# The factors of the second and the final RMSNorm as rows through DRAM, in place of diagonals and products with ones

## The chip, the cores and the metric

The kernel runs on one core of a Trainium2 chip. The metric is the device time of one execution in microseconds (us), of which a median over several executions is given. The engines are named as in the profile: PE is TensorE (PEld its weight loads), DVE is VectorE, ACT is ScalarE, POOL is GpSimd, and SP is SyncE, which issues most of the DMA transfers.

## The reference

One layer for 2048 prompt tokens and 64 sample tokens of width 1024, all in float32. What matters here are the second and the final norm; the first half of the layer is cut to a line.

```python
def rmsnorm(x, g):
    xf = x.astype(jnp.float32)
    y = xf * lax.rsqrt(jnp.mean(xf * xf, -1, keepdims=True) + EPS)
    return y * g.astype(jnp.float32)

def layer(...):
    ...                       # norm 1, projection, pooling mixer and mLSTM, output projection
    x = x + gt1 * mix
    h2 = rmsnorm(x, g2) * (1 + sc2) + sh2
    up = h2 @ w_up
    ...                       # causal depthwise convolution of width 3, then
    x = x + gt2 * ((jax.nn.silu(g) * a) @ w_down)

y = rmsnorm(x, g_final)
```

Each norm has one factor for each token, the reciprocal root of a mean over the 1024 features.

## The kernel before

Activations lie with features on the 128 partitions and tokens along the free axis, so a norm's factor must be multiplied along the free axis, the same row on every partition. Products are made from float32 values split into a high and a low part, which is why a matmul often comes three times.

The first half of the layer goes over four token groups of 512 (the last has 576, with the sample tokens). In it a scheduler sets the order of each engine's instructions from the order in which they are written and their dependencies. The second half, the FFN, goes over three groups of 704 tokens, each seen as two halves of 352 (FH). There the order of PE, ACT, DVE and POOL is the order in which the instructions are written, and SP's is the scheduler's.

Side work is written as Python generators in lists (bg[0] to bg[4], and side). Each `yield` is a place to stop, and a product calls tick(0) twice, each call advancing the first generator by one step. A product of the FFN is twelve matmuls of 352 columns. So the number of yields sets where in the row of products a step of side work stands.

Every engine works its own row in order. A tile that two operations share makes the later one wait for the earlier.

The steps that the change and the prediction name:

- `rstd_rows` (the sum of squares turned into factors for token groups 0 to 2) and `stat2` with `rstd_cols` (for group 3) leave the second norm's factors as columns in RS2: 128 tokens on the partitions, one column for each tile of 128 tokens. `final` does the same for the final norm in RF, by `stat_cols`.
- `bcast_cols` turns columns into a row that stands on all partitions: DVE multiplies the identity by the factors (L687, L692), ACT and DVE split the result into a high and a low part (L696, L697), PE multiplies both by a matrix of ones, two matmuls for each 352 tokens (L702, L703), and ACT copies the result out of PSUM into rb (L704).
- `normed` multiplies by rb and the gain on DVE (L714) and adds the shift on ACT (L717).
- `norm_h` makes the normed input of FFN group 0 during the last token group: it loads x from DRAM (x2d, L727), in 16 pieces of 352 tokens, and stores the result (h2d). `prepare` does so for FFN groups 1 and 2, inside the FFN of the group before.
- `final` multiplies the eight tiles of a group's result by rb (L1911) and stores them to yT (L1915). `load_x2` (L1883) then refills these tiles from x2d for the next group, and the down-projection adds into them (L2010). The last group has its own ending, which the change leaves alone.
- Around norm_h, the last token group has `proj_v` (weights w_v, products L1129, evictions gt on DVE and va on ACT, both by a helper at L233), the work on w_ada (L210, on DVE) and the splitting of weights into high and low parts (L394 on ACT, L397 on DVE).
- In the FFN, L1595 is the up-projection, L1604 and L1608 take its results from PSUM, L1568 and L1573 are the convolution, L1642 and L1725 are other evictions on ACT, L2038 and L2161 are down-projections.

Of the kernel before, what the change touches and what calls it, by code (L numbers as in the profile page):

```python
# [9 lines left out]
F32 = mybir.dt.float32  # L10
# [55 lines left out]
def tile_layer(ctx: ExitStack, tc: tile.TileContext, xT, vecs, cst, rst, w_mod, w_ada, c_rows, w_qkou, w_v, w_pool,  # L66
# [443 lines left out]
    def rstd_rows(ssum, o, out, done):  # L510
# [18 lines left out]
        done.append(1)  # L529

# [26 lines left out]

    def modulate(dst, x, k, rb, G, sh, o):
# [12 lines left out]
    pool.memset(RS2, 0.0)  # L571
    RF = cp.tile([P, 6], F32, tag="RF", name="RF")
    pool.memset(RF, 0.0)
# [19 lines left out]
    def stat2(o, ssum):  # L593
        out = RS2[:, 4 * o.g:4 * o.g + len(o.chunks)]
        for _ in range(12):
            yield
        rstd_cols([ssum], o, out)
        yield

    def outproj(o, mix, between):  # L600
# [75 lines left out]
    def bcast_cols(rs, t0, w, box, scr, r0=0):  # L676

        rb = scr("rb")
        dg, dh, dl = scr(), scr(F32R), scr(F32R)
        t = t0  # L680
        while t < t0 + w:
            c, a = divmod(t, P)
            n = 1
            if a == 0 and t + P <= t0 + w:
                n = (t0 + w - t) // P
                v = dg[:, t - t0:t - t0 + n * P].rearrange("p (t c) -> p t c", c=P)
                dve.tensor_tensor(out=v, in0=ident.unsqueeze(1).broadcast_to([P, n, P]),  # L687
                                  in1=rs[:, c:c + n].unsqueeze(2).broadcast_to([P, n, P]), op=ALU.mult)
                t += n * P
            else:  # L690
                e = min(P, a + t0 + w - t)
                dve.tensor_scalar(out=dg[:, t - t0:t - t0 + e - a], in0=ident[:, a:e], scalar1=rs[:, c:c + 1],  # L692
                                  scalar2=None, op0=ALU.mult)
                t += e - a
        yield
        act.activation(dh[:, :w], dg[:, :w], AF.Copy)  # L696
        dve.tensor_tensor(out=dl[:, :w], in0=dg[:, :w], in1=dh[:, :w].bitcast(F32), op=ALU.subtract)  # L697
        yield
        yield
        for lo in range(0, w, FH):  # L700
            ps = m2_ps()
            pe.matmul(ps[:, :FH], ones_r, dh[:, lo:lo + FH], start=True, stop=False)  # L702
            pe.matmul(ps[:, :FH], ones_r, dl[:, lo:lo + FH], start=False, stop=True)  # L703
# [1612 lines left out]
```

## Time and profile before

| | |
|---|---|
| runs | 2162.03, 2164.13, 2164.81 us; median 2164.13 |
| the profiled execution's own time | 2170.81 us |
| its span | 2169.0 us |
| granted TensorE clock, mean | 0.998 |
| busy: PE, PEld | 2143.5, 2042.9 us |
| busy: DVE, ACT, POOL | 1629.1, 1096.2, 250.5 us |
| DMA | 543.63 MB, mean 251 GB/s |

Durations come from the profiled execution. A timeline's row has the start, the length, the engine, the line, what is written and read, a count, and in brackets the idle time before it with what ended it. A matmul's own duration is its latency; how much of PE's row it takes is read from the starts of its neighbours. DMA rows have the size of one transfer and the median time from issue to landing.

### The profile page before, as it was taken

How to read it: one execution, taken by the hardware profiler on the slowest of the kernel's cores; microseconds unless marked ns; L12 is line 12 of the kernel's file. 1: busy time of each engine (PE TensorE's matmuls, PEld its weight loads, DVE VectorE, ACT ScalarE, POOL GpSimd, SP SyncE). 2: the span in 40 equal slices, each digit the busy share in tenths (PEclk: the TensorE clock that was granted, in tenths of full speed). 3: DMA queues.
4: the chain of work that ended last, by engine and by line, in shares of the span. 5: the costliest groups of instructions: out<-in, count | busy, mean ns of one | idle time of the engine just before them, and what ended most of it. 6: DMA issues, size and time to landing. Idle time of an engine off the chain costs nothing.

```text
span 2169.0 us, 37946 instructions
## 1 busy us (share of the span) xinstructions
PE 2143.5 (99%) x13488; PEld 2042.9 (94%) x13488; DVE 1629.1 (75%) x3068; ACT 1096.2 (51%) x2182; POOL 250.5 (12%) x499
## 2 busy tenths in 40 slices
PE   8999999999999999999999999999999999999998
PEld 7788988888899999999999999999999999999998
DVE  5678768767964868797957668988876597887874
ACT  4555235334333546464736455655655365565554
POOL 0000000002000101010101120100100331111112
PEclk9999999999999999999999999999999999999999
DMA  8897998988886576889977976666678675555542
GB/s 306 305 327 256 336 338 279 354 319 292 279 306 221 168 261 219 303 279 313 331 225 244 322 265 196 229 224 199 221 232 264 217 260 183 174 174 189 174 160 79
DMA packets 245862, 543.63 MB, mean 251 GB/s; under 512 B 25252, under 2 KB 68772, under 8 KB 242856
## 3 DMA queue, kind: packets, MB, share of 16 engines
q1 hardware_dynamic: 236232, 518.89, 70.6%
q10 hardware_dynamic: 9440, 22.32, 2.6%
q8 instruction: 106, 1.74, 0.3%
q14 instruction: 84, 0.69, 0.1%
HBM read 415.12 MB, written 125.99 MB: 249 GB/s over the span
## 4 chain that ended last, share of the span: by engine, by line
PE 71%; DVE 8%; DMA 4%; issue 2%; ACT 2%; SPq 0%; POOL 0%; DVEq 0%; POOLq 0%; ACTq 0%
PE mm L1595 33%; PE mm L460 14%; PE mm L2161 12%; PE mm L2038 8%; DVE wt L397 2%; DMA wt<-wsum 1%; PE mm L1129 1%; DMA raw<-w_ada 1%; DVE tg L1573 1%; ACT tg L1568 0%; PE m L1350 0%; PE m L1330 0%; PE m L1352 0%; DVE scr L233 0%; DMA wsum<-w 0%
## 5 line engine op out<-in xcount | busy, mean ns | idle before, releaser
L1595 PE MATMUL mm<-hx,wt 128*128 128x352 f32 x5544 | 888.6, 321 | 1.6 <-DVE eg L1604 1.6
L1595 PEld LDWEIGHTS mm<-hx,wt 128*128 128x128 f32 x5544 | 881.9, 188 | 2.9 <-ACT wt L394 1.3
L460 PE MATMUL mm<-hl,wt 128*128 128x512 f32 (+2 forms) x1920 | 388.4, 357 | 0.8 <-ACT va L233 0.8
L394 ACT ACTIVATE wt<-raw 128x512 fp32r<-128x512 f32 (+3 forms) x470 | 276.8, 597 | 169.6 <-PE mm L2161 47.7
L460 PEld LDWEIGHTS mm<-hl,wt 128*128 128x128 f32 x1920 | 315.7, 189 | 43.9 <-ACT va L233 1.0
L397 DVE TENSOR_TENSOR wt<-raw,wt 128x512 fp32r<-128x512 f32 (+3 forms) x470 | 312.7, 671 | 47.8 <-ACT wt L394 47.0
L2161 PE MATMUL mm<-av,wt 128*128 128x448 f32 (+1 forms) x1632 | 262.7, 322 | 0.0
L2161 PEld LDWEIGHTS mm<-av,wt 128*128 128x128 f32 x1632 | 250.4, 188 | 11.1
L2010 DVE SCALAR_TENSOR_TENSOR x<-mm,MOD,x 128x352 f32<-128x352 f32 (+3 forms) x360 | 167.4, 504 | 78.6 <-PE mm L2161 65.1
L2038 PE MATMUL mm<-av,wt 128*128 128x352 f32 x1344 | 220.8, 323 | 2.5 <-DVE ea L1604 0.9
L2038 PEld LDWEIGHTS mm<-av,wt 128*128 128x128 f32 x1344 | 215.4, 188 | 5.6 <-DVE ea L1604 3.6
L1642 ACT ACTIVATE mm<-mm 128x352 f32<-128x352 f32 x196 | 87.8, 448 | 250.3 <-PE mm L1595 194.0
L460 PE MATMUL mm<-mx,wt 128*128 128x512 f32 (+1 forms) x960 | 183.1, 352 | 0.4 <-DVE scr L233 0.3
L460 PEld LDWEIGHTS mm<-mx,wt 128*128 128x128 f32 x960 | 159.4, 189 | 23.3 <-issue 0.5
L1573 DVE SCALAR_TENSOR_TENSOR ta<-ea,V,ta 128x704 f32<-128x704 f32 (+1 forms) x132 | 125.7, 952 | 64.4 <-ACT ta L1568 51.6
L1573 DVE SCALAR_TENSOR_TENSOR tg<-eg,V,tg 128x704 f32<-128x704 f32 (+1 forms) x132 | 125.7, 952 | 62.0 <-ACT tg L1568 59.7
L397 DVE TENSOR_TENSOR wt<-wt 128x512 fp32r<-128x512 f32 x196 | 132.8, 684 | 12.9 <-ACT wt L394 12.9
L394 ACT ACTIVATE wt<-wt 128x512 fp32r<-128x512 f32 x196 | 119.8, 623 | 36.2 <-DMA wt<-wsum 32.0
L1551 POOL COPY ea<-UC 128x2 f32<-128x2 f32 x66 | 32.9, 499 | 484.8 <-DVE ta L1573 397.0
L1782 ACT ACTIVATE tg<-tg 128x704 f32<-128x704 f32 (+1 forms) x66 | 52.5, 795 | 71.2 <-DVE tg L1573 71.2
L1129 PE MATMUL mm<-wt,hl 128*128 128x256 f32 (+1 forms) x576 | 71.1, 284 | 0.0
L1129 PEld LDWEIGHTS mm<-wt,hl 128*128 128x128 f32 x576 | 70.3, 190 | 0.6 <-issue 0.4
(298 smaller groups left out, 2173.5 us busy)
## 6 DMA issues: line engine op xcount, KB each, us to landing
wt<-wsplit SPq DMA_DIRECT2D x132, 512.0 KB, 4.5
raw<-w_up SPq DMA_DIRECT2D x198, 256.0 KB, 4.0
wt<-hl_kept SPq DMA_DIRECT2D x96, 512.0 KB, 5.9
wt<-wsum SPq DMA_DIRECT2D x132, 256.0 KB, 4.9
wsplit<-wt SPq DMA_DIRECT2D x66, 512.0 KB, 5.5
w<-w_up SPq DMA_DIRECT2D x44, 512.0 KB, 5.1
wsum<-w SPq DMA_DIRECT2D x22, 1024.0 KB, 4.8
Bd<-fscr ACTq DMA_DIRECT2D x56, 352.0 KB, 4.3
```

Of the source, the lines that this page charges most:

```text
L394: act.activation(u.w[:, 0, :u.n], u.raw[:, :u.n], AF.Copy)
L397: dve.tensor_tensor(out=u.w[:, 1, :u.n], in0=u.raw[:, :u.n], in1=u.w[:, 0, :u.n].bitcast(F32), op=ALU.subtract)
L460: pe.matmul(ps[bi][:, :hi - lo], U[:, a, k % 4 * P:(k % 4 + 1) * P], mv[k][:, b, lo:hi], start=(at == 0 and pi == 0), stop=(k == order[-1] ...
L1129: pe.matmul(ps[ti][:n, :cols], h[4 * kh + k4][:, b, lo:lo + n], U[:, a, k4 % 2 * cols:(k4 % 2 + 1) * cols], start=(kh == 0 and k4 == 0 and ...
L1551: pool.tensor_copy(ext[:, 0:2], UC[:, f, :])
L1573: dve.scalar_tensor_tensor(out=t[:, :E], in0=ext[:, j:j + E], scalar=wc(j, f), in1=t[:, :E], op0=ALU.mult, op1=ALU.add)
L1595: pe.matmul(bk.t[:, :FH], U[:, a, kc * P:(kc + 1) * P], Bo.at(nm, kc, b), start=(first and kc == 0 and pi == 0), stop=(kc == 3 and pi == 2 ...
L1642: act.activation(to.t[:, :FH], bk.t[:, :FH], AF.Copy)
L1782: act.activation(self.tg[:, :E], self.tg[:, :E], AF.Silu)
L2010: dve.scalar_tensor_tensor(out=x3[n][:, a:b], in0=bk.t[:, a - lo:b - lo], scalar=gt2(n, s), in1=x3[n][:, a:b], op0=ALU.mult, op1=ALU.add)
L2038: pe.matmul(bk.t[:, :FH], U[:, a, c:c + P], quad.put(op, m, b), start=(first and m == 0 and pi == 0), stop=(m == 1 and pi == 2), skip_grou ...
L2161: pe.matmul(bks[i].t[:, :hi - lo], U[:, a, k % 4 * P:(k % 4 + 1) * P], av[k][:, b, lo:hi], start=(k == 0 and (a, b) == PASSES[0]), stop=(k ...
```

## The change

The factors, as columns, are transposed by PE into a small tile with tokens along the free axis, copied out of PSUM by DVE and stored to DRAM by ACT's DMA queue (`row_out`). Where they are wanted, one DMA, issued by ACT, reads that row with stride zero into all 128 partitions (`spread_row`). Diagonals, splits, products with ones and the copies of their results go, and with them the two clears of RS2 and RF. `norm_h` is now advanced to its first yield before `proj_v` of the last token group; it waits three yields after its rows, as does `prepare`. `final` waits five yields between the store and the load, and five between the load and the first use.

```diff
...
                               op0=ALU.mult, op1=ALU.add)
             pool.tensor_tensor(out=out[:n, a:b], in0=out[:n, a:b], in1=half[:n, :b - a], op=ALU.pow)
         done.append(1)
+        if to is not None:
+            yield
+            yield
+            row_out(to, out, token_tiles(o), scr)
 
     def bcast(rs, o, box):
 
...
         box.append(rb)
         yield
 
+    def row_out(to, cols, tiles, new):
+
+        pt, R, t = m2_ps(), new(), 0
+        for i, (c, n, w) in enumerate(tiles):
+            pe.transpose(pt[:c, i * P:i * P + n], cols[:n, t:t + c], ident[:n, :n])
+            dve.tensor_copy(R[:c, i * P:i * P + n], pt[:c, i * P:i * P + n])
+            act.dma_start(out=to[w:w + c * n].rearrange("(c p) -> c p", p=n), in_=R[:c, i * P:i * P + n])
+            t += c
+
+    def token_tiles(o):
+        return [(b - a, n, a * P) for (a, b, n, s) in o.tsegs]
+
+    def spread_row(out, rd, t0, w):
+
+        act.dma_start(out=out[:, :w], in_=rd[t0:t0 + w].unsqueeze(0).broadcast_to([P, w]))
+
     def modulate(dst, x, k, rb, G, sh, o):
         t = scr()
         for (a, b, s) in o.segs:
...
     h2d = dr.tile([KD, P, FT], F32, tag="h2d", name="h2d")
     Bd = dr.tile([len(BN), 4, P, 2, FH], F32, tag="Bd", name="Bd")
     RS2 = cp.tile([P, NCH], F32, tag="RS2", name="RS2")
-    pool.memset(RS2, 0.0)
     RF = cp.tile([P, 6], F32, tag="RF", name="RF")
-    pool.memset(RF, 0.0)
+    r2d = dr.tile([NTOK], F32, tag="r2d", name="r2d")
 
     def load_x(k, o):
         x = scr()
...
         for _ in range(12):
             yield
         rstd_cols([ssum], o, out)
+        for _ in range(4):
+            yield
+        row_out(r2d[o.t0:o.t0 + o.T], out, token_tiles(o), fscr)
         yield
 
     def outproj(o, mix, between):
...
         if o.last:
             bg[0].append(stat2(o, ssum))
         else:
-            side.append(rstd_rows(ssum, o, RS2[:, 4 * o.g:4 * o.g + len(o.chunks)], []))
+            side.append(rstd_rows(ssum, o, RS2[:, 4 * o.g:4 * o.g + len(o.chunks)], [], r2d[o.t0:o.t0 + o.T]))
 
     fgroups = []
     for g in range(NFG):
...
                 self.make(nm, kc // 2)
             return self.tiles[nm, kc // 2][:, kc % 2, part, HO:HO + FH]
 
-    def bcast_cols(rs, t0, w, box, scr, r0=0):
-
-        rb = scr("rb")
-        dg, dh, dl = scr(), scr(F32R), scr(F32R)
-        t = t0
-        while t < t0 + w:
-            c, a = divmod(t, P)
-            n = 1
-            if a == 0 and t + P <= t0 + w:
-                n = (t0 + w - t) // P
-                v = dg[:, t - t0:t - t0 + n * P].rearrange("p (t c) -> p t c", c=P)
-                dve.tensor_tensor(out=v, in0=ident.unsqueeze(1).broadcast_to([P, n, P]),
-                                  in1=rs[:, c:c + n].unsqueeze(2).broadcast_to([P, n, P]), op=ALU.mult)
-                t += n * P
-            else:
-                e = min(P, a + t0 + w - t)
-                dve.tensor_scalar(out=dg[:, t - t0:t - t0 + e - a], in0=ident[:, a:e], scalar1=rs[:, c:c + 1],
-                                  scalar2=None, op0=ALU.mult)
-                t += e - a
-        yield
-        act.activation(dh[:, :w], dg[:, :w], AF.Copy)
-        dve.tensor_tensor(out=dl[:, :w], in0=dg[:, :w], in1=dh[:, :w].bitcast(F32), op=ALU.subtract)
-        yield
-        yield
-        for lo in range(0, w, FH):
-            ps = m2_ps()
-            pe.matmul(ps[:, :FH], ones_r, dh[:, lo:lo + FH], start=True, stop=False)
-            pe.matmul(ps[:, :FH], ones_r, dl[:, lo:lo + FH], start=False, stop=True)
-            act.activation(rb[:, lo:lo + FH], ps[:, :FH], AF.Copy)
-        box.append(rb)
-        yield
-
-    def normed(x, k, t0, w, rb, steps=(0, 1)):
+    def normed(x, k, t0, w, rb, steps=(0, 1), pin=lambda i: i):
 
         for (a, b, s) in ((t0, min(t0 + w, TP), 0), (max(t0, TP), t0 + w, 1)):
             if a < b:
                 a, b = a - t0, b - t0
                 if 0 in steps:
-                    dve.scalar_tensor_tensor(out=x[:, a:b], in0=x[:, a:b], scalar=G2[:, k, s:s + 1], in1=rb[:, a:b],
-                                             op0=ALU.mult, op1=ALU.mult)
+                    pin(dve.scalar_tensor_tensor(out=x[:, a:b], in0=x[:, a:b], scalar=G2[:, k, s:s + 1], in1=rb[:, a:b],
+                                                 op0=ALU.mult, op1=ALU.mult))
                 if 1 in steps:
-                    act.activation(x[:, a:b], x[:, a:b], AF.Identity, bias=sh2(k, s))
+                    pin(act.activation(x[:, a:b], x[:, a:b], AF.Identity, bias=sh2(k, s)))
 
     def norm_h(o, rows, scr):
 
...
             load(i)
         box = []
         for h in range(2):
-            yield from bcast_cols(RS2, o.t0 + h * FH, FH, box, lambda dt=F32: rows[10 + h] if dt == "rb" else scr(dt))
+            box.append(rows[10 + h])
+            spread_row(box[h], r2d, o.t0 + h * FH, FH)
+        for _ in range(3):
+            yield
         for i, (t0, k) in enumerate(todo):
-            normed(xs[i], k, t0, FH, box[i // KD])
+            normed(xs[i], k, t0, FH, box[i // KD], pin=tc.keep_in_program_order if i == 0 else lambda i: i)
             nc.sync.dma_start(out=h2d[k, :, t0:t0 + FH], in_=xs[i])
             yield
             if i > 1 and i + 6 < len(todo):
...
     def prepare(o, scr):
 
         box = []
-        yield from bcast_cols(RS2, o.t0, FT, box, scr)
-        yield
+        box.append(scr("rb"))
+        spread_row(box[0], r2d, o.t0, FT)
+        for _ in range(3):
+            yield
         for kc in range(4):
             for _ in range(2 if kc else 0):
                 yield
...
                     cols = []
                     va = proj_v(o, h, cols)
             else:
+                if o.last:
+                    xs = [t[:, j * FH:(j + 1) * FH] for t in [big(mx_tile(k)) for k in range(4)] for j in range(3)]
+                    ahead_h = norm_h(fgroups[0], xs, scr)
+                    next(ahead_h)
                 cols = []
                 va = proj_v(o, h, cols)
             if o.g == 0:
...
                 dve.tensor_copy(E_r, t[:P, :NH])
             if o.g == 0:
                 bg[3].append(ada(2, quarter))
-            if o.last:
-                xs = [t[:, j * FH:(j + 1) * FH] for t in [big(mx_tile(k)) for k in range(4)] for j in range(3)]
-            elif o.g:
+            if o.g and not o.last:
                 xs = rows_of(groups[o.g + 1])
             mix = [None] * NH + [mx_tile(NH + hd) for hd in range(NH)]
             box, hn = [], []
...
                 bg[0].append(lstm(o, hd, qko, va, cols, mix[4 + hd]))
                 if hd == 0:
                     if o.last:
-                        bg[1].append(norm_h(fgroups[0], xs, lambda dt: sp.tile([P, TMAX], dt, tag="scr", name="scr")))
+                        bg[1].append(ahead_h)
                     else:
                         bg[1].append(norm1(groups[o.g + 1], xs, box))
             drain(3)
...
         yield
         yield
         box = []
-        yield from bcast_cols(RF, 0, FT, box, fscr)
         yield
         yield
+        rd = dr.tile([FT], F32, tag=f"rf{o.g}", name=f"rf{o.g}")
+        nf, rest = divmod(FT, P)
+        row_out(rd, RF, [(nf, P, 0), (1, rest, nf * P)], fscr)
+        for _ in range(5):
+            yield
+        box.append(fscr("rb"))
+        spread_row(box[0], rd, 0, FT)
+        for _ in range(5):
+            yield
         for k in range(KD):
             dve.scalar_tensor_tensor(out=x3[k], in0=x3[k], scalar=V[:, V_GF + k:V_GF + k + 1], in1=box[0],
                                      op0=ALU.mult, op1=ALU.mult)
...
```

Three places in the order of the instructions. First SP, at the start of the last token group; x2d read into an mx tile is a load of norm_h, x2d written from scr is a store of the first half's result. Before:

```order
L196 DMA raw<-w_ada 128x512 x3
L727 DMA mx_6210<-x2d 128x352
L623 DMA x2d<-scr 128x512
L196 DMA raw<-w_ada 128x512
L727 DMA mx_6210<-x2d 128x352
L373 DMA raw<-w_v 128x512
L727 DMA mx_6210<-x2d 128x352
L373 DMA raw<-w_v 128x512
L727 DMA mx_6211<-x2d 128x352 x2
```

And now:

```order
L196 DMA raw<-w_ada 128x512 x3
L717 DMA mx_5846<-x2d 128x352
L645 DMA x2d<-scr 128x512
L717 DMA mx_5846<-x2d 128x352 x2
L717 DMA mx_5847<-x2d 128x352 x3
L717 DMA mx_5848<-x2d 128x352 x2
L834 DMA w_5870<-w_up 128x1024
L645 DMA x2d<-scr 128x512
L834 DMA w_5870<-w_up 128x1024
L196 DMA raw<-w_ada 128x512
L373 DMA raw<-w_v 128x512 x2
```

All eight first loads of norm_h, and two loads of w_up, stand ahead of the last two loads of w_v, where three of norm_h's did. On DVE, at about the same place, the row before is work on w_ada, one split of a w_v weight and the first gt of proj_v:

```order
L210 ISA MOD 128x1
L210 ISA raw,MOD<-raw,s_6029,V 128x512
L210 ISA MOD 128x1
L397 TENSOR_TENSOR wt<-raw,wt 128x512
L210 ISA junk,MOD<-raw,s_6028,MOD 128x512
L210 ISA MOD 128x1
L210 ISA raw,MOD<-raw,acc,MOD 128x512
L210 ISA MOD 128x1
L233 COPY gt<-mm 128x2x4
```

And now, with seven of the sixteen operations of `normed` (L714 before, L704 now) in one run:

```order
L210 ISA raw,MOD<-raw,acc,MOD 128x512
L210 ISA MOD 128x1
L704 SCALAR_TENSOR_TENSOR mx_5846<-mx_5846,G_110,mx_5849 128x352 x2
L704 SCALAR_TENSOR_TENSOR mx_5847<-mx_5847,G_110,mx_5849 128x352 x3
L704 SCALAR_TENSOR_TENSOR mx_5848<-mx_5848,G_110,mx_5849 128x352 x2
L210 ISA junk,MOD<-raw,u,V 128x512
L210 ISA MOD 128x1
L210 ISA raw,MOD<-raw,s_6052,V 128x512
L210 ISA MOD 128x1
L397 TENSOR_TENSOR wt<-raw,wt 128x512
L233 COPY gt<-mm 128x2x4
```

The run of normed operations stands ahead of the splits of the last two w_v weights and of the first gt; before, the first of them came after proj_v had ended. The third place is `final` of FFN group 0, PE first; L1902 and L1899 are the sums over features. Before:

```order
L1902 MATMUL m_13585<-ones_r,ssum 128x1 x5
L1902 MATMUL m_13585<-ones_r,ssum 64x1
L1595 MATMUL mm<-hx,wt 128x352 x30
L702 MATMUL m_13646<-fscr,ones_r 128x352
L703 MATMUL m_13646<-fscr,ones_r 128x352
L702 MATMUL m_13650<-fscr,ones_r 128x352
L703 MATMUL m_13650<-fscr,ones_r 128x352
L1595 MATMUL mm<-hx,wt 128x352 x348
```

And now:

```order
L1899 MATMUL m_13572<-ones_r,ssum 128x1 x5
L1899 MATMUL m_13572<-ones_r,ssum 64x1
L1592 MATMUL mm<-hx,wt 128x352 x24
L566 MATMUL m_13620<-V,RF 5x128
L566 MATMUL m_13620<-V,RF 1x64
L1592 MATMUL mm<-hx,wt 128x352 x354
```

The two transposes stand 24 matmuls behind the sums, and the products with ones stood 30 behind. On ACT, there, before:

```order
L696 ACTIVATE fscr<-fscr 128x704
L1608 ACTIVATE ea<-mm 128x352
L704 ACTIVATE rb<-m_13646 128x352
L704 ACTIVATE rb<-m_13650 128x352
L394 ACTIVATE wt<-raw 128x512
L1642 ACTIVATE mm<-mm 128x352
```

And now:

```order
L1605 ACTIVATE ea<-mm 128x352
L568 DMA rf_13619<-fscr 5x128
L568 DMA rf_13619<-fscr 1x64
L394 ACTIVATE wt<-raw 128x512
L576 DMA rb<-rf_13619 128x704
L1639 ACTIVATE mm<-mm 128x352
```

The spread is one row behind the two stores that it reads, ahead of the eviction that was L1642 and is L1639.

More of the change, by code (lines that the diff above doesn't have):

```diff
@@ L508, in rstd_cols, with rstd_rows @@
             pool.tensor_tensor(out=out[:n, a:b], in0=out[:n, a:b], in1=half[:n, :b - a], op=ALU.pow)
-    def rstd_rows(ssum, o, out, done):
+    def rstd_rows(ssum, o, out, done, to=None):
         pt, R = m2_ps(), scr()
```

## The prediction

> **What bounds the kernel now.** I read the page's head first, then busy time by stretches, then the waits of TensorE, then timelines at the places that the change touches.
>
> ```profile
> span 2169.0 us, 37946 instructions
> PE 2143.5 (99%) x13488; PEld 2042.9 (94%) x13488; DVE 1629.1 (75%) x3068; ACT 1096.2 (51%) x2182; POOL 250.5 (12%) x499
> ```
>
> TensorE is busy for 2143.5 of 2169.0 us. VectorE has a quarter of its time free, ScalarE half. So this change is priced in matmuls taken out of TensorE's row, and in waits put into it. The stretches (columns: length, then the busy us of PE, PEld, DVE, ACT and POOL with counts, granted clock, DMA share, GB/s) say how full that row is:
>
> ```profile
> 400.00:780.00 380.00, 378.38 (x2516) 350.36 (x2516) 275.87 (x623) 155.89 (x402) 34.62 (x64) 1.00 0.79 274
> 1100.00:1400.00 300.00, 299.93 (x1897) 296.74 (x1896) 218.24 (x342) 158.99 (x288) 39.33 (x65) 1.00 0.75 251
> 2150.00:2169.00 19.00, 11.49 (x93) 10.82 (x92) 9.17 (x26) 4.19 (x10) 5.72 (x8) 0.88 0.41 152
> ```
>
> Between 1100 and 1400, where eight of the twenty removed matmuls lie, TensorE idles 0.07 us; between 400 and 780, where four lie, 1.6 us. A slot saved there is saved, and a wait put there is paid. The other waits that are left:
>
> ```profile
> PE m L1330 <- DVE kw L233: 3.8, 3, 2.7
> PE mm L1595 <- DVE eg L1604: 1.6, 2, 1.1
> ```
>
> The profiled execution took 2170.81 us, 1.8 more than its span and 6.7 above the median of the runs, 2164.13. The sum below is a difference made in the profiled execution's durations; I put it on the median.
>
> **Part one: the twenty matmuls with ones go.** Four for the two halves of norm_h, eight for prepare of FFN groups 1 and 2, eight for the final norm of groups 0 and 1. Here is one block of four on TensorE:
>
> ```profile
> 1256.19 0.79 PE L1902 MATMUL m<-ones_r,ssum 128*128 128x1 f32 x6
> 1256.91 5.03 PE L1595 MATMUL mm<-hx,wt 128*128 128x352 f32 x30
> 1261.77 0.32 PE L702 MATMUL m<-fscr,ones_r 128*128 128x352 f32 x1
> ...
> 1262.25 0.32 PE L703 MATMUL m<-fscr,ones_r 128*128 128x352 f32 x1
> 1262.41 0.79 PE L1595 MATMUL mm<-hx,wt 128*128 128x352 f32 x4
> ```
>
> The rows show 0.32 us for one, but that is latency: four of them occupy 1261.77 to 1262.41, so 0.16 each, and no row carries a wait. Twenty are worth 20 x 0.16 = 3.2 us. The Trainium skill, page "TensorE: Matmul & The Clock Gate", section "Back-to-back issue gap", gives N/2.4 GHz plus some 2.5 ns, which for 352 columns is an estimate of 149 ns; by it the term would be 3.0 us. The row is this kernel's own and decides.
>
> The diagonals on DVE and their splitting on ACT and DVE go too, as do ten ACT copies and two clears on POOL. None of them is on TensorE, and no wait of TensorE in these stretches is put down to them. I price them at nothing. What covers them is TensorE's own full row; were that cover gone they would be gains, not costs.
>
> **Part two: nine transposes come.** One each in rstd_rows of token groups 0 to 2, and two each in stat2 and in the final norm of groups 0 and 1. Their prices come from rows of the same kinds:
>
> ```profile
> 616.54 0.71 PE L1225 MATMUL m<-V,R 128*128 128x128 f32 x5
> 617.09 0.27 PE L521 MATMUL m<-V,scr 128*128 128x128 f32 x1
> 597.74 0.29 DVE L516 COPY scr<-m 128x128 f32<-128x128 f32 x1
> 1257.01 0.22 DVE L1892 TENSOR_SCALAR RF<-m 128x5 f32<-128x5 f32 x2 [4.88 <-PE m L1902]
> 1257.26 2.13 POOL L1894 TENSOR_TENSOR RF<-RF,half 128x5 f32<-128x5 f32 x2 [3.00 <-DVE RF L1892]
> 617.64 1.38 POOL L528 TENSOR_TENSOR RS<-RS,half 128x4 f32<-128x4 f32 x1 [15.97 <-DVE RS L526]
> 625.36 0.71 PE L1305 MATMUL m<-V,k 128*128 128x128 f32 x5
> ```
>
> Five transposes of 128 columns hold TensorE from 616.54 to 617.09: 0.11 each, so nine are 1.0 us. Do they find their operand ready? In token group 2 (the new row stands behind L1315, which follows L1305 at 625.36) the factors are done at 619.0, six us before. In final the powers end at 1259.39; the transposes stand 24 matmuls behind the sums, 24 x 0.16 = 3.9 us after 1256.91, at 1260.8. Ready, with 1.4 us to spare.
>
> Where row_out has two tiles, both transposes write one PSUM tile, and the order has the second wait for DVE's copy of the first: a round trip on TensorE, three times. One costs the first transpose's latency 0.27, the hand-over (L1902 ends at 1256.98 and DVE starts at 1257.01: 0.03; I take 0.05 for the way back), and the copy 0.29, less the 0.11 already counted: 0.53. DVE must be free for that:
>
> ```profile
> 1257.00:1261.00 4.00, 4.00 (x26) 4.00 (x27) 2.05 (x6) 2.04 (x4) 2.70 (x4) 1.00 0.12 46
> ```
>
> It is busy 2.05 of the 4 us before the place, part of that with the diagonals that go. So three trips are 1.6 us. Bounds: nothing, if the weights queue hides it; 1.5 us each if a 0.95 us operation of DVE stands in the way, 4.4 in all. I take 1.6. The single transposes in the token groups have nothing to wait for. Their copies stand among DVE's work for kw and st, for which TensorE waited 3.8 us above; 0.29 us each, at most 0.9 more, taken as nothing because kw stands ahead of the copy.
>
> **Part three: nine small stores and six broadcast loads come**, all issued by ACT.
>
> ```profile
> Bd<-fscr ACTq DMA_DIRECT2D x56, 352.0 KB, 4.3
> raw<-w_down SPq DMA_DIRECT2D x16, 64.0 KB, 2.5
> s<-cs SPq DMA_DIRECT2D x8, 256.0 KB, 5.1
> mx<-x2d SPq DMA_DIRECT2D x16, 176.0 KB, 4.5
> 1266.41 0.45 ACT L1642 ACTIVATE mm<-mm 128x352 f32<-128x352 f32 x1 [2.78 <-PE mm L1595]
> 1269.72 1.94 DVE L1573 SCALAR_TENSOR_TENSOR ta<-ea,V,ta 128x704 f32<-128x704 f32 x2 [0.74 <-issue]
> ```
>
> For prepare and norm_h the store was made long before; only in the final norm does the load follow its own store. The spread waits for the store on ACT's queue, ahead of L1642. The store goes out at about 1262.2 (1260.8 plus 1.4 us for both transposes and copies) and lands 2.5 to 4.3 later, at 1264.7 to 1266.5; ACT would have stood idle until 1266.41 anyway, so it is held 0.1 us at most. The broadcast, as s<-cs, takes 5.1: 1271.6 at the latest. The first use of rb now stands behind the two L1573, which end at 1271.66. So the term is nothing, with 0.1 us of slack. It is thin, but it is DVE's slack; the eg and ea that TensorE needs next stand ahead. If the load takes 2 us more, DVE is 2 us late in a stage where it is idle a quarter of the time. The stores to yT move six ticks later (a product of twelve matmuls has two) and pass SP's queue later; the x tiles that they free are wanted only in the next down-projection.
>
> **Part four: norm_h is started earlier.** Its row goes ahead of proj_v of the last token group, so eight x2d loads, with one store among them, stand on SP ahead of the last two w_v loads, and seven normed operations stand in a row on DVE and on ACT, before the gt copies and va evictions of proj_v, which used to come some 60 us before them.
>
> ```profile
> raw<-w_v SPq DMA_DIRECT2D x16, 256.0 KB, 6.2
> 566.58 0.33 SPq L727 DMA_DIRECT2D mx<-x2d  x1
> 570.45 1.58 SPq L373 DMA_DIRECT2D raw<-w_v  x1
> 573.62 0.63 ACT L394 ACTIVATE wt<-raw 128x512 fp32r<-128x512 f32 x1 [4.36 <-DMA raw<-w_v]
> 581.75 0.75 DVE L210 CUSTOM_DVE_ANT_0 junk<-raw,s,MOD 128x512 f32<-128x512 f32 x1 [2.48 <-DMA raw<-w_ada]
> 583.23 0.16 DVE L233 COPY gt<-mm 128x8 f32<-128x8 f32 x1
> 583.42 0.39 ACT L233 ACTIVATE va<-mm 128x256 f32<-128x256 f32 x1 [4.88 <-DVE gt L233]
> 585.73 4.96 PE L1129 MATMUL mm<-wt,hl 128*128 128x256 f32 x40
> 598.90 0.68 ACT L233 ACTIVATE scr<-scr 4x576 f32<-4x576 f32 x1 [5.91 <-DVE scr L233]
> 602.16 4.14 PE L460 MATMUL mm<-hl,wt 128*128 128x320 f32 x29 [0.80 <-ACT va L233]
> L714 DVE SCALAR_TENSOR_TENSOR mx<-mx,G,mx x15: 569/582/585, 643.2 to 669.7; 128x352 f32<-128x352 f32 x15
> 565.00:585.00 20.00, 20.00 (x142) 18.91 (x141) 16.05 (x40) 4.11 (x8) 0.00 (x0) 1.00 0.91 301
> 585.00:605.00 20.00, 19.20 (x163) 18.50 (x162) 19.25 (x49) 6.09 (x13) 1.40 (x2) 1.00 0.88 295
> ```
>
> The two w_v loads, which went out between 569 and 572, now also stand behind two w_up loads of 512 KB. I estimate that they go out 3 to 4 us later, 574.5, and with 6.2 to land arrive at 580.7. By then DVE is still at the normed operations, so this delay hides behind the next one.
>
> Seven at 0.58 are 4.1 us. Between 565 and 585 DVE has 20 - 16.05 = 3.95 us free, nearly as much; between 585 and 605 it has 0.75. But the first normed needs its row, which cannot land before 566.58 + 4.5 + 5.1 = 576.2, and part of the free time lies before that. I estimate a quarter of it unusable, so DVE leaves this place about 1 us late. At va the first bank is read by 583.8 and wanted at 585.73: 1.9 us of slack cover it. The late DVE shows where no slack is left: its scr feeds ACT at 598.90, the va evictions stand behind that on ACT, and TensorE already waits 0.80 us for them at 602.16. So the term is +1.0. Bounds: 0, if all the idle time takes up work, and 4.7, if none does and one normed of 0.58 falls among the va. I take the low part because the idle rows (2.48 on w_ada) are waits for loads that the same queue brings anyway.
>
> **Sum:** -3.2 + 1.0 + 1.6 + 0 + 1.0 = +0.4 us, that is 2164.5. A measurement of this kernel can tell about 0.2%, 4.3 us, from no change, so "same" runs from 2159.8 to 2168.5.
>
> **The rivals.**
>
> *Slower by the start of the last token group.* DMA engines are 0.91 busy there. If the first x2d or the spread row comes 2 us later than its median, DVE stands with the ada work, the last two w_v units and gt behind it, and the delay is 4.7 plus part of these 2. With 1.9 us of slack at va gone and the wait at 602 fully exposed, it is +5.5 in place of +1.0: 2169. It decides from a normed that starts after about 578. For it: DVE's 19.25 of 20 behind. Against it: the 3.95 us ahead. The last stretch of the trace, where TensorE idled 7.5 of 19 us, was granted a clock of 0.88, so a long stall could cost 0.12 of what follows, some 2 us in 19: 2171. The Trainium skill, same page, section "HAM oscillation — how this bites in real kernels", puts the point where the clock falls at idle gaps of some 3.4 us; only this rival reaches such a gap.
>
> *Faster: the matmuls' whole price comes through.* If the round trips are hidden, and the freed DVE time takes away waits, it is -3.2 + 1.0 and the removal of 0.8, 1.6 and part of the 3.8: between -2.2 and -6, about 2159. For it: everything removed was work. Against it: the waits on kw and eg lie nowhere near the removed operations.
>
> *The row comes late in final.* If store and load together need over 11 us, DVE is held at L1911 beyond what its idle quarter takes up, twice; with ta and eg of the next product behind it TensorE would lose what lies above that, 2 to 3 us each: 2169 to 2170. It needs a pair of transfers 2 us slower than any median above, while the stretch just before has a DMA share of 0.12.
>
> **How the numbers follow.** Forecast, the sum within its small bounds: 0.68. Slow start of the group: 0.15. Row late in final: 0.05. Faster: 0.12. The faster rival lies just outside 0.2%, the slower ones too, so faster 0.12, same 0.68, slower 0.20. The range takes in the near edge of both sides: 2159.5 to 2169.5.
>
> **What would show it.** TensorE's count falls by 11; each pair of transposes in stat2 and final shows an idle of about 0.5 us released by DVE, and the single ones none. DVE's busy time falls by some 8 us and ACT's by some 9, with the end unmoved. The seven normed lie between 576 and 582, and the wait for va near 602 is about 1.8 us. I am wrong if that wait is above 4, if TensorE's stretches with the removed blocks shrink by more than their slots, or if rows of L1911 begin with a wait for a DMA over 2 us.

## The result, and the profile after

The changed kernel is slower: median 2175.16 us against 2164.47 for the kernel before in the same comparison, ratio 1.0043, 95% interval 1.003 to 1.0056. That is 9.3 us (6.5 to 12.1; the medians alone lie 10.7 apart, the figure that the expectations below use); the forecast was 2164.5, and the measured time lies above the range that was given. Below, "above before" is a ratio less one, times 2164.5, with its interval worked out in the same way.

The head of the page after:

```profile
span 2173.5 us, 37905 instructions
PE 2143.1 (99%) x13477; PEld 2040.7 (94%) x13477; DVE 1621.2 (75%) x3058; ACT 1088.4 (50%) x2166; POOL 248.1 (11%) x497
```

The instruction counts came as forecast: 11 fewer matmuls, DVE 7.9 us less busy, ACT 7.8 less. But the span is longer, and the busy time of TensorE hardly fell though 20 matmuls went and 9 transposes came. Its waits, in the stretches 400 to 800 and 800 to 2140 (us in total, times, longest):

```profile
PE m L1345 <- DVE st L233: 2.3, 1, 2.3
PE mm L460 <- ACT va L233: 1.3, 1, 1.3
PE mm L1124 <- ACT va L233: 1.2, 2, 0.9
...
PE mm L2043 <- DVE ea L1601: 2.8, 2, 1.9
PE m L566 <- DVE fscr L567: 1.4, 3, 0.5
```

The wait on eg of 1.6 us that before had is down to 0.2. New are va at L1124 and L566, and st, which was 0.2; the one on ea has grown from 0.9. And in two places TensorE was granted half its clock (columns as in the stretches before; clock, DMA share and GB/s at the end):

```profile
636.40:639.80 3.40, 3.32 (x15) 3.32 (x16) 3.40 (x10) 1.09 (x4) 0.00 (x0) 0.50 0.91 351
1571.70:1575.00 3.30, 3.30 (x13) 3.30 (x12) 3.30 (x7) 1.22 (x3) 0.20 (x1) 0.50 0.33 99
```

TensorE is busy in both, and in the second makes 13 matmuls where the kernel before makes 23 in the same time, ten fewer of 158 ns each, so this half-clock stretch costs some 1.6 us that no wait shows.

The profiled execution of before, at 2170.8 us, was itself a high one. A second profile of the unchanged kernel was therefore taken:

> The kernel before, unchanged, for a second profile of it. The first, at 2170.8 us, was 6.3 us above its median; I expect about 2164 here, without the slow stretch of matmuls between 1601 and 1658 (2.8 us) that the first has, and without its half-clock stretch near 79 (1.7 us).

It took 2163.67 us (span 2161.9), close to the median, and had neither of the two slow places. Its waits between 400 and 800 are all below 1 us. Against it the span of after is 11.6 us longer, close to the difference of the medians, 10.7. I matched the matmuls of the two traces one by one and read how far the same matmul starts later. Up to 440 it is 0.9. At 632, behind st and the half-clock stretch, 6.5: the start of the last token group costs 5.6. Then 0.7 is won at norm_h's matmuls, and again 0.7 at each place where a block of four is gone. Each pair of transposes loses about 1 us, the first half of the second FFN group about 2, the place around ea near 1560 another 2.0, and its half-clock stretch 1.6, of which 0.6 is won back right behind it. Two costs are large, then: the start of the last token group, and something that moved the evictions in the FFN. The second is not in the prediction at all.

### The profile page after: what moved, and what is told of

Its sections match the earlier page's. It is cut to its first block, busy times and chain, and to the rows that moved or that the text cites. A ratio compares the mean times of both kernels' runs of the same rounds, so it can differ in the third digit from the quotient of the medians.

```text
span 2173.5 us, 37905 instructions
## 1 busy us (share of the span) xinstructions
PE 2143.1 (99%) x13477; PEld 2040.7 (94%) x13477; DVE 1621.2 (75%) x3058; ACT 1088.4 (50%) x2166; POOL 248.1 (11%) x497
## 3 DMA queue, kind: packets, MB, share of 16 engines
q8 instruction: 106, 1.74, 0.3%
## 4 chain that ended last, share of the span: by engine, by line
PE 77%; DVE 5%; DMA 2%; issue 1%; ACT 1%; SPq 0%; POOL 0%; DVEq 0%; POOLq 0%; ACTq 0%
PE mm L1592 37%; PE mm L460 16%; PE mm L2166 12%; PE mm L2043 8%; PE mm L1124 1%; DVE wt L397 1%; DMA wsum<-w 1%; PE m L1345 1%; PE m L1347 1%; DVE tg L1570 0%; DVE fscr L704 0%; PE m L1325 0%; DMA mx<-x2d 0%; ACT tg L1565 0%; PE m L1310 0%
## 5 line engine op out<-in xcount | busy, mean ns | idle before, releaser
L1639 ACT ACTIVATE mm<-mm 128x352 f32<-128x352 f32 x196 | 87.8, 448 | 256.5 <-PE mm L1592 198.8
L1124 PE MATMUL mm<-wt,hl 128*128 128x256 f32 (+1 forms) x576 | 71.5, 285 | 1.2 <-ACT va L233 1.2
L1124 PEld LDWEIGHTS mm<-wt,hl 128*128 128x128 f32 x576 | 70.4, 190 | 2.3 <-ACT va L233 1.7
```

The costliest lines, as they stand in the source:

```text
L1124: pe.matmul(ps[ti][:n, :cols], h[4 * kh + k4][:, b, lo:lo + n], U[:, a, k4 % 2 * cols:(k4 % 2 + 1) * cols], start=(kh == 0 and k4 == 0 and ...
L1639: act.activation(to.t[:, :FH], bk.t[:, :FH], AF.Copy)
```

## The experiments

Theory A: the time goes into waits of TensorE at places where DVE's work was moved, and into the half-clock stretches behind them. Theory B: the added transfers cost time in themselves, by traffic or by queue time, wherever DVE's work stands.

**1. norm_h started at its old place.** The lines ahead of proj_v go, and the generator is made where it was:

```diff
-                    ahead_h = norm_h(fgroups[0], xs, scr)
-                    next(ahead_h)
...
-                        bg[1].append(ahead_h)
+                        bg[1].append(norm_h(fgroups[0], xs, scr))
```

> The changed kernel with norm_h started at its old place, behind proj_v of the last token group; rows through DRAM everywhere, as changed. Theory A (waits put where DVE's work moved): the new waits at va (1.2 us at L1124, 0.5 more at the wait near 602) and at st (2.3 us) go, and with them the half-clock stretch of 3.4 us that stands behind the wait at st (1.7 us lost): 5.7 us less than the changed kernel, so about 5 us above the kernel before. Theory B (the added transfers themselves cost, by traffic or by queue time): 10.7 us above before, as changed, give or take 1.

Measured: 2173.23, ratio 1.0043 (1.0031 to 1.0055), 9.3 above before: nothing gained that can be told. The waits at L1124 and st did go. Another took their place (timelines of DVE, ACT and PE):

```profile
592.00 0.59 DVE L704 SCALAR_TENSOR_TENSOR mx<-mx,G,mx 128x352 f32<-128x352 f32 x1 [3.15 <-DMA mx<-r2d]
...
599.78 0.68 ACT L233 ACTIVATE scr<-scr 4x576 f32<-4x576 f32 x1 [2.12 <-DVE scr L233]
...
603.04 1.18 PE L460 MATMUL mm<-hl,wt 128*128 128x320 f32 x4 [1.88 <-ACT va L233]
```

Now DVE stands 3.15 us for the row from DRAM right behind proj_v, normed operations stand ahead of the gates' scr, and va is late behind it. TensorE waits 1.88 us and a half-clock stretch follows at 603. Since the rows come without matmuls, the old place in the code is no longer the old place on DVE: what had kept the first normed operation until 643 was the matmuls with ones, which stood at 642.0 in TensorE's row. A's arithmetic failed here, and the rows show what took the place of the waits that went; B is not shown by it.

**2. The normed operations in program order, loads still early.**

```diff
-            normed(xs[i], k, t0, FH, box[i // KD], pin=tc.keep_in_program_order if i == 0 else lambda i: i)
+            normed(xs[i], k, t0, FH, box[i // KD], pin=tc.keep_in_program_order)
```

> The changed kernel with all sixteen normed operations of norm_h kept in program order: the eight x2d loads stay early on SP, but the seven normed operations leave the place ahead of gt and va. Theory A with DVE's row as the cause: the waits at va (1.2 us) go as in late_h; the wait at st stays if it comes from w_up behind the early loads and stores on SP, and goes if it comes from DVE. Time between 5 and 10.7 above before. Rival: the early loads on SP alone are what delays w_v and w_ada, then the waits at va stay.

Measured: 2170.53, ratio 1.0027 (1.0018 to 1.0037), 5.8 above before, about 3.5 less than the changed kernel, though the two intervals overlap. The waits at L1124 are gone, st fell to 1.1, and between 20 and 2150 the profile has no half-clock stretch at all. By the expectation this would say that DVE's row made va late at L1124. But DVE's rows ahead of the first gt say otherwise (the changed kernel first, then this one):

```profile
576.80 3.56 DVE L704 SCALAR_TENSOR_TENSOR mx<-mx,G,mx 128x352 f32<-128x352 f32 x7 [3.14 <-DMA mx<-r2d]
581.59 0.75 DVE L210 CUSTOM_DVE_ANT_0 junk<-raw,u,V 128x512 f32<-128x512 f32 x1 [1.23 <-DMA raw<-w_ada]
...
583.67 0.16 DVE L233 COPY gt<-mm 128x8 f32<-128x8 f32 x1
```

```profile
581.59 0.75 DVE L210 CUSTOM_DVE_ANT_0 junk<-raw,u,V 128x512 f32<-128x512 f32 x1 [6.88 <-DMA raw<-w_ada]
...
583.67 0.16 DVE L233 COPY gt<-mm 128x8 f32<-128x8 f32 x1
```

Without the seven operations DVE waits for the same w_ada load, which SP issues behind the early loads, and the first gt comes at the same time. TensorE needs its result at 585.22 here; in the changed kernel it would have at 583.37 (584.30 less a wait of 0.93). Experiments 5 and 8 keep the seven ahead of gt, wait for the same load, and have no wait at L1124. So DVE's row is not shown as the cause there. The rows speak for the load, which is a cost by queue time, though of loads that were moved and not added; and whether TensorE then waits at L1124 differs from one execution to the next. What the edit is seen to change is st and the clock behind it.

**3. Two yields more in prepare.** Before, bcast_cols and the yield behind it made five; the change has three.

```diff
         spread_row(box[0], r2d, o.t0, FT)
-        for _ in range(3):
+        for _ in range(5):
             yield
```

> The changed kernel with two more yields in prepare ahead of its first load, so that its normed operations stand again where they stood before, behind eg and ea at the change from up- to down-projection. Theory A: the wait of 1.9 us for ea near 1570 and the half-clock stretch behind it (1.7 us) go; a wait of 1.1 us for eg near 1067, which the changed kernel does not have, may come back: 2.5 to 3.6 us less than the changed kernel, 7 to 8 above before. Theory B: 10.7 above before.

Measured: 2168.02, ratio 1.0013 (1.0005 to 1.0022), 2.8 above before. This is the largest gain of any mending, 6.5 us, more than expected, and its interval lies clear of the changed kernel's. Here is DVE around the end of the up-projection: before, after, and with five yields.

```profile
1563.17 0.52 DVE L1604 TENSOR_TENSOR eg<-mm,s 128x352 f32<-128x352 f32 x1
1563.61 0.51 DVE L1604 TENSOR_TENSOR ea<-mm,s 128x352 f32<-128x352 f32 x1
...
1566.24 1.07 DVE L714 SCALAR_TENSOR_TENSOR fscr<-fscr,G,rb 128x640 f32<-128x640 f32 x2
```

```profile
1564.53 1.07 DVE L704 SCALAR_TENSOR_TENSOR fscr<-fscr,G,rb 128x640 f32<-128x640 f32 x2
...
1566.12 1.07 DVE L704 SCALAR_TENSOR_TENSOR fscr<-fscr,G,rb 128x640 f32<-128x640 f32 x2
...
1569.51 0.52 DVE L1601 TENSOR_TENSOR eg<-mm,s 128x352 f32<-128x352 f32 x1
1569.94 0.52 DVE L1601 TENSOR_TENSOR ea<-mm,s 128x352 f32<-128x352 f32 x1
...
1570.52 1.23 PE L2043 MATMUL mm<-av,wt 128*128 128x352 f32 x6 [1.89 <-DVE ea L1601]
```

```profile
1563.71 0.52 DVE L1601 TENSOR_TENSOR eg<-mm,s 128x352 f32<-128x352 f32 x1
1564.15 0.52 DVE L1601 TENSOR_TENSOR ea<-mm,s 128x352 f32<-128x352 f32 x1
...
1566.78 1.08 DVE L704 SCALAR_TENSOR_TENSOR fscr<-fscr,G,rb 128x640 f32<-128x640 f32 x2
```

Two ticks, one product of twelve matmuls, decide whether four normed operations (2.1 us) stand ahead of the two evictions that free TensorE's PSUM banks, or behind them. By the matched matmuls its trace is 6.0 us shorter than the changed kernel's from 640 on: 1.6 in the first FFN group, the rest in the second, with 2.0 at ea, 1.6 in the half-clock stretch (0.6 of it won back right behind), and a few tenths at each earlier block.

**4. The same two ticks in the kernel before.** The gain of experiment 3 could also come from the row's having longer to land. So the kernel before, which fetches no row, got two yields less:

```diff
-    def bcast_cols(rs, t0, w, box, scr, r0=0):
+    def bcast_cols(rs, t0, w, box, scr, r0=0, two=True):
...
-        yield
-        yield
+        yield
+        if two:
+            yield
...
-        yield from bcast_cols(RS2, o.t0, FT, box, scr)
-        yield
+        yield from bcast_cols(RS2, o.t0, FT, box, scr, two=False)
```

> The kernel before with two yields less in prepare, so that its normed operations stand two ticks earlier, at the places where the changed kernel has them; diagonals and products with ones stay. Theory A (the place of normed between the evictions eg and ea costs what the two yields gave back, 7.1 us): 5 to 8 us above the kernel before, with a wait for ea of about 1.9 us near 1570. Rival (the two yields helped because the row, fetched from DRAM, had two ticks more to land): no change here, within 1.5 us of before.

Measured: 2171.03, ratio 1.003 (1.002 to 1.0041), 6.5 above before. Its waits between 800 and 2140:

```profile
PE mm L2038 <- DVE ea L1604: 2.8, 2, 1.9
PE m L704 <- DVE fscr L697: 0.9, 1, 0.9
```

The wait on ea is the changed kernel's to the digit, without any row. The place of normed is shown as the cause, and theory B falls for this part. The 0.9 at its L704 is this experiment's own: the split now comes too shortly ahead of the products with ones, and by the matched matmuls that place costs about 1.1. The size rests on the times, 6.5 (4.3 to 8.9), and less on this one profile: against the second profile of before it loses 3.1 us between 640 and 1600, with no half-clock stretch there, and 3.3 ahead of 640, at waits for kw that the edit does not touch.

**5. norm_h alone changed**, with prepare, stat2 and final as before. From the changed kernel, with bcast_cols and the two clears back:

```diff
-            side.append(rstd_rows(..., [], r2d[o.t0:o.t0 + o.T]))
+            side.append(rstd_rows(..., [], r2d[o.t0:o.t0 + o.T] if o.g < 2 else None))
...
-        spread_row(box[0], r2d, o.t0, FT)
...
+        yield from bcast_cols(RS2, o.t0, FT, box, scr)
+        yield
...
-        spread_row(box[0], rd, 0, FT)
...
+        yield from bcast_cols(RF, 0, FT, box, fscr)
```

> The kernel before with norm_h alone changed: rows through DRAM for token groups 0 and 1, norm_h started ahead of proj_v; prepare, stat2 and final keep diagonals and products with ones. Theory A: the waits at va and st and the half-clock stretch appear as in the changed kernel (5.7 us by 632 against the second profile of before), less the four matmuls of norm_h (0.6): 4 to 6 us above before. If most of the 10.7 us is prepare's two ticks (6.5 us, shown apart), this and that must add up to about the whole.

Measured: 2168.31, ratio 1.0017 (1.0008 to 1.0026), 3.7 above before. The waits at L1124 did not appear in this profile; st did, with the half-clock stretch behind it:

```profile
PE m L1374 <- DVE st L233: 2.5, 1, 2.5
```

What DVE waited for there (the kernel before first, then this one):

```profile
632.72 0.69 DVE L849 TENSOR_TENSOR w<-w 128x512 f32<-128x512 f32 x1 [2.63 <-DMA w<-w_up]
```

```profile
632.14 0.69 DVE L873 TENSOR_TENSOR w<-w 128x512 f32<-128x512 f32 x1 [4.94 <-DMA w<-w_up]
...
633.47 0.34 DVE L233 SCALAR_TENSOR_TENSOR st<-SP,GL,m 128x129 f32<-128x129 f32 x1
```

A sum of w_up weights, background work that nobody needs soon, waits for its load at the head of DVE's row, and the states st that TensorE needs stand behind it. Before, the load was late too, but TensorE had work until then. With norm_h early, its stores to h2d and its further loads of x2d run at the same time as this load (in the changed kernel SP issues five of them from 628.4 to 632.8, right behind the w_up load at 627). From its issue to the end of DVE's wait the load takes 6.5 us here and 7.4 in the changed kernel; in the two profiles of before it lands in 4.6 and 4.9. That this traffic is the reason is argued, not shown. In experiment 1 four stores to h2d run beside the same load and DVE has it after 4.7 us, so the stores alone don't do it.

**6. norm_h alone, normed in program order.** The edit of experiment 2 on top of 5, so that those stores come later.

> As only_h (norm_h alone changed), with its sixteen normed operations kept in program order, so that none of them stands ahead of gt and va, and their stores to h2d go out later. If it is the place of the normed operations (and of the stores that follow them) that makes the wait of 2.5 us at st and the half-clock stretch behind it, both go, and the four matmuls saved are seen: 2163 to 2164.5, level with the kernel before. If the eight early loads on SP alone do it, it stays 4 us above before with st waiting above 2 us.

Measured: 2166.71, ratio 1.0012 (1.0002 to 1.0022), 2.6 above before. In the profile it went as expected: st is down to 0.3, and the clock between 600 and 640 is whole again, with the DMA engines less busy (the wait, then the stretch, that of experiment 5 first):

```profile
PE m L1374 <- DVE st L233: 0.3, 1, 0.3
```

```profile
600.00:640.00 40.00, 37.25 (x271) 36.53 (x270) 27.01 (x65) 13.66 (x47) 3.55 (x9) 0.96 0.92 336
```

```profile
600.00:640.00 40.00, 38.75 (x290) 37.84 (x291) 25.64 (x64) 12.85 (x45) 4.89 (x10) 1.00 0.85 310
```

The time did not come level with before, as it should have. The two intervals, of 5 and of 6, overlap. The other profiles agree on st: with the seven normed operations early it waits 1.9 to 2.9 us in four of them, with all sixteen in program order 0.3 to 1.5 in five, and before at most 0.2. So that the place of the normed operations makes st later is shown by the rows; how it delays the w_up load, and that it is all of norm_h's price, isn't.

**7. final alone changed.** From the kernel before, with row_out and spread_row added:

```diff
-        yield from bcast_cols(RF, 0, FT, box, fscr)
         yield
         yield
...
+        row_out(rd, RF, [(nf, P, 0), (1, rest, nf * P)], fscr)
...
+        spread_row(box[0], rd, 0, FT)
+        for _ in range(5):
+            yield
```

> The kernel before with final alone changed, for FFN groups 0 and 1. Per group the four matmuls go (0.64 us) and the two transposes with their round trip come (0.88 us on TensorE in the changed kernel's profile): 0.5 us above before for both, no difference that can be told. Rival (rows late, yT stores and x loads behind): a wait for x at the first down-projection sums, 1 us or more above before.

Measured: 2165.35, ratio 1.0006 (0.9997 to 1.0014), 1.3 above before, no difference that can be told. The wait for x of 0.7 is there, but before has the same.

The three parts alone are 3.7, 1.3 and, by experiment 4, 6.5. They add to 11.5 against 9.3 (6.5 to 12.1) for the whole. The 6.5 is on the high side for prepare's part of the change: experiment 4 keeps the eight matmuls that the change takes out of prepare (1.3 us), and has about 1.1 us of its own at L704. The rows of stat2 and rstd_rows were not changed alone.

**8. No round trip.** Both transposes ahead of both copies:

```diff
             pe.transpose(pt[:c, i * P:i * P + n], cols[:n, t:t + c], ident[:n, :n])
+            t += c
+        for i, (c, n, w) in enumerate(tiles):
             dve.tensor_copy(R[:c, i * P:i * P + n], pt[:c, i * P:i * P + n])
             act.dma_start(out=to[w:w + c * n].rearrange("(c p) -> c p", p=n), in_=R[:c, i * P:i * P + n])
-            t += c
```

> The changed kernel with both transposes of a row_out written ahead of both copies, so that the second does not wait for the first copy. Theory A: the three waits of 0.5 us at L566 go, 1.6 us less than the changed kernel, 9 above before. Theory B: 10.7 above before. At most one us apart, so the waits of TensorE at L566 in the profile decide, not the time.

Measured: 2175.16, ratio 1.0052 (1.004 to 1.0064), 11.3 above before. The waits at L566 are gone from the profile, and the pair takes 0.34 us where it took 0.88:

```profile
1265.48 0.41 PE L566 MATMUL m<-V,RF 128*5 128x128 f32 x2
1265.82 2.49 PE L1593 MATMUL mm<-hx,wt 128*128 128x352 f32 x14
```

The time did not fall. In that one trace TensorE runs two long stretches at a slower pace (the last section), 2.5 and 1.7 us longer than the changed kernel's, more than the 1.6 to be gained. Whether the other executions have them was not seen, so the gain is shown in the rows and not in the time.

**9 to 11. Mendings together.** First the edits of 2 and 3; then with norm_h also at its old place; then 2, 3 and 8.

> The changed kernel with the two yields in prepare and with norm_h's normed operations in program order. If the two costs are separate they add: 10.7 - 7.1 - 4.6, about 1 us below the kernel before (2163.5). If both only took the same stall's half-clock stretch away, about 2 us above it.

> As the one before, and norm_h started at its old place, behind proj_v. If the eight early x2d loads on SP still cost (they delay w_ada, w_v and w_up), this is 1 to 2 us faster than the one before, 2162; if DVE's row was all of it, the same within 1 us. The new wait of 1.9 us near 602, which starting late alone had, should be gone, since the normed operations no longer stand ahead of the gate's scr.

> The changed kernel with all three mendings: two yields more in prepare, norm_h's normed in program order, both transposes of row_out ahead of both copies. Against the version with the first two (2165.8) the three round trips of 0.54 us go: 2164.2, level with the kernel before. The matmuls saved (3.2 less 1.0 for transposes) would make 2162.3 if nothing else stood against them.

Measured: 2165.77, ratio 1.0005 (0.9996 to 1.0014); 2167.69, ratio 1.0015 (1.0006 to 1.0024); 2168.89, ratio 1.0016 (1.0005 to 1.0027). The first brings the change level with before: 1.1 above, and its interval holds no difference. It had been expected 1 us below. The costs add nearly as they were measured apart. Starting norm_h late on top of it gains nothing (3.2 above before; the wait for va near 602, which had been expected to go, is 1.2), so the eight early loads cost nothing that can be told by time. And taking the round trips out as well is, again, no gain (3.5 above before, expected level). No version here beats the kernel before.

## Why the prediction was wrong, point by point

- **The step that failed first is one that is not in the sum.** Part two and three price what prepare no longer does and what it loads; nothing prices that its normed operations start two ticks earlier. The change took five yields down to three. Experiments 3 and 4 put 6.5 us on that by time, in both directions; of it their profiles show 6.0 and 3.1. Of the removed work the prediction says "None of them is on TensorE, and no wait of TensorE in these stretches is put down to them. I price them at nothing." It follows DVE's order for norm_h and for final, and not for prepare.
- **Part four's +1.0 was mis-sized.** The start came nearly as told: the first normed operation started at 576.80, waiting 3.14 us for its row (told: not before 576.2), and the seven took 3.56 us (told: 4.1, with 0.58 for each; in a row they start 0.50 apart):

```profile
576.80 3.56 DVE L704 SCALAR_TENSOR_TENSOR mx<-mx,G,mx 128x352 f32<-128x352 f32 x7 [3.14 <-DMA mx<-r2d]
583.67 0.16 DVE L233 COPY gt<-mm 128x8 f32<-128x8 f32 x1
636.48 0.80 PE L1345 MATMUL m<-st,q 128*128 128x129 f32 x2 [2.33 <-DVE st L233]
```

  What failed next is the overlap "By then DVE is still at the normed operations, so this delay hides behind the next one." DVE was done with them at 580.36, and the loads came later, w_ada at 581.57 and w_v at 582.3 (told 580.7); it was the normed operations that lay inside the wait for a load. The first gt came 0.44 us later than in the first profile of before, but TensorE wanted its result 2.4 us sooner (583.37 against 585.73), so the 1.9 us of slack was gone. By the matched matmuls 1.8 us were lost at L1124, told as 0, and 0.8 at the wait near 602, told as 1.0. The largest piece was elsewhere: 2.9 at st and in the half clock behind it, 34 us further on, from a w_up load that the prediction does not follow. In all 5.6 us in this trace; norm_h's part alone is 3.7 (1.7 to 5.6) by time, with its four matmuls already won.
- **The slower rival** named this place and allowed for the clock, but its point of decision (a normed start after 578) wasn't reached, and it ended on va rather than st. It came nearest, at a chance of 0.15.
- **The removed matmuls** were right: each block of four is worth 0.7 us in the matched traces, 0.64 told.
- **The round trips** were right in kind and size. Told were 0.53 each beyond the transposes; TensorE's idle is 0.46, and pair and trip together take 804.40 to 805.28, 0.88 us:

```profile
804.40 0.27 PE L566 MATMUL m<-V,RS 128*4 128x128 f32 x1
805.14 0.21 PE L566 MATMUL m<-V,RS 64*1 64x64 f32 x1 [0.46 <-DVE fscr L567]
805.28 0.90 PE L1592 MATMUL mm<-hx,wt 128*128 128x352 f32 x4
```

- **The store and load in final** were right: DVE's use of rb (L1916) shows no idle before it, and experiment 7 finds no difference.
- **The clock.** The prediction allowed it in a rival only, and set it beside a gap of some 3.4 us from the Trainium skill, page "TensorE: Matmul & The Clock Gate", section "HAM oscillation — how this bites in real kernels". The runs do not agree with that gap as a threshold: waits of 1.9 to 2.9 us were followed by the drop (the last section).

## What to carry to other kernels

Where side work is stepped by yields, the number of yields is part of the schedule: after a change, read for each generator which engine's rows have swapped places with the evictions that free PSUM, even where the generator has only lost work. Work that is taken out may have been what held other work back; look for what now comes early. On an engine that works in order, ask of each background operation ahead of the critical one what transfer it waits for, and what new traffic runs beside that transfer.

## What the runs showed that was not expected

**Half clock behind short waits.** Leaving out the start and the end, the profiles have eight waits of TensorE of 2.3 us or more (2.33 to 2.87). At seven of them, at kw near 78 or at st near 634, there is a 3.4 us stretch at clock 0.50; at the eighth, 2.83 us for w_out in experiment 6, there is none. Waits of about 1.9 us had it in three cases (ea in the changed kernel, st in experiment 3, va in experiment 1) and not in six others, four at ea and two at kw near 122. Shorter ones never had it. So it isn't the length alone that decides.

It is where the wait falls. In all fourteen profiles every change of the clock stands on a grid of 3.413 us (in experiment 8's the two drops at 78.69 and 638.48 are 164 steps apart), and the grid lies differently against the program in each execution. Take TensorE's idle time in each step of that grid between 20 and 2150. The ten steps with 1.82 us of it or more are each followed by one step at half clock; no step with 1.74 or less is. In the changed kernel the 1.89 us at ea lay in one step, 1568.23 to 1571.64. In experiments 1, 2, 4 and 8 a border cut the same wait, and no step had more than 1.63 of idle time there. The 2.83 us for w_out were cut into 1.44 and 1.39. So the same wait at ea costs 1.6 us more in one execution and nothing more in the next.

**Two paces at full clock.** At a granted clock of 1.00 and with no idle time, TensorE takes 158 ns a matmul of 352 columns in most stretches and 167 in some. The same 40 us in the two profiles of the unchanged kernel (matmuls in brackets behind PE's busy time):

```profile
1605.00:1645.00 40.00, 40.00 (x242) 40.00 (x241) 27.78 (x40) 23.87 (x42) 4.70 (x12) 1.00 0.69 230
```

```profile
1605.00:1645.00 40.00, 40.00 (x255) 40.00 (x254) 27.97 (x40) 24.01 (x42) 3.65 (x12) 1.00 0.75 255
```

The stretch from 1601 to 1658 costs 2.8 us where it is slow, one from about 800 to 855 costs 2.5. The two profiles of the unchanged kernel differ in which they have, and the kernels of experiments 7 to 11 had one or two long ones in their profiles. Between the two profiles of the unchanged kernel, 7.1 us apart, this (2.8) and a longer wait for kw near 78 with the half clock behind it (3.1) make up most. What sets the pace was not found.
